# Output rows read back in five and three head pairs, and the last half row tile in two quarters

## The chip, the cores and the metric

The kernel runs on one core of one Trainium2 chip. The metric is the device time of one execution in microseconds (us), shown as the median of several runs. One execution is also recorded by the hardware profiler; the trace and the profile page come from it.

## The reference

The kernel computes a trunk of two hybrid encoder layers on 1024 rows of 1024 columns. Three groups of attention heads (A, B, C) run on column slices of one projection; each group's output is multiplied by its gate, all are joined to 1024 columns, and one output projection maps them back. A last RMSNorm closes the trunk.

```python
def rms_norm(x, g):
    y = xf * lax.rsqrt(jnp.mean(xf * xf, axis=-1, keepdims=True) + EPS)
    return (y * g.astype(jnp.float32)).astype(x.dtype)
...
    oc = mla_blocks(qc_nope, qc_rope, kc_nope, kc_rope, vc, (C_NOPE + C_ROPE) ** -0.5) * jax.nn.silu(cg)
    o = jnp.concatenate([oa, ob, oc], axis=-1)
    return x + jnp.einsum('bsm,md->bsd', o, w_out)
...
    return rms_norm(h, final_g)
```

The change lies in the `einsum` with `w_out` (for both layers) and in the last `rms_norm`.

## The kernel before

**Precision.** A product of two float32 matrices is made as three matmuls in a rounded format: each operand is split into a high part (a cast) and a low part (a subtraction), and high × high, high × low and low × high are added in PSUM (`mm3`, L133 to L136). So every tile that is multiplied needs a cast, mostly on ACT or POOL, and a subtraction on DVE, before it can be used in full.

**The output projection.** Attention writes its results to a scratch array in HBM, `d_o`, in eight head pairs of 128 (A 0 to 2, B 3 to 5, C 6 and 7). The projection reads them back by row tile `st` of 128 rows (eight of them): `out_rows` (L1016) loads some pairs of one tile, or of two, into `ol`; `out_hl` (L1025) makes the high part `oh` on ACT (L1029) and turns `ol` into the low part on DVE (L1030). In the kernel before a row tile has pairs 0 to 5 in one tile (768 columns, two buffers) and pairs 6 and 7 of two row tiles in another (one buffer). The weights Wo are eight tiles, one for a head pair, each loaded in two halves `wost` and split into `woh` and `wol` (`load_wo`, L1041): 0 to 4 (`MW = 5`) during the last part of attention, 5 to 7 in a second pool when attention's keys have been given up (L1219). For each row tile and each half of 512 output columns, `out_part` (L1053) adds 8 pairs × 3 matmuls into one PSUM tile `pw`.

**What runs when.** `ab_done` (L997) runs while group C's last units are still under way. It loads row tiles 0 and 1 and Wo's first five tiles, and the first four `out_part`s, pairs 0 to 4, are woven into the end of attention as filler work (L1209). Behind that the loop over row tiles (L1227) finishes these halves with pairs 5 to 7, adds the residual `y` on DVE (L1238), loads row tile `st + 2`, and in layer 0 begins the next layer's norm, in layer 1 the last RMSNorm.

**The end of attention.** The last group of C (`c_1_6`, rows 6 and 7 of head pair 7) makes two products with the values, `poc_1_6_0_1` and `poc_1_6_1_1` (16 matmuls of 256 columns each), in one PSUM bank, the O bank: `pv` (L752) multiplies, ACT copies half of the bank (`ohc`, L763), and DVE adds the other half to it (`oc`, L1156). Only then is the bank free for the next product. The finished group is multiplied by its gate on POOL and written to `d_o` (`finish`, L1121).

**What sets the order.** Each engine works through its own list in order, and waits on semaphores. Where the code doesn't pin two instructions to each other, a scheduler with a model of the times chooses the order in each list when the kernel is built (`schedule_with_timeline_sim=True`, L1346). All loads and stores without an engine of their own go through SP's queue (L97); `queue_behind` (L98) keeps them behind a given earlier one. Behind Wo's last half, SP is given the broadcast of the next norm's weights (`ng`; in the last layer `fg`, 128 copies of a row, 512 KB) and the loads for the row tiles from 2 on.

Of the kernel before, what the change touches and what calls it, by code (L numbers as in the profile page):

```python
# [8 lines left out]
F32 = mybir.dt.float32  # L9
F32R = mybir.dt.float32r  # L10
AF = mybir.ActivationFunctionType
ALU = mybir.AluOpType
# [4 lines left out]
EPS = 1e-6  # L17
# [8 lines left out]
MW = 5  # L26
# [19 lines left out]
def kernel(  # L46
# [21 lines left out]
    nc = tc.nc  # L68
    P = 128
    S, D = x.shape[1], x.shape[2]  # L70
    DEPTH = norm_g.shape[0]
    NS = S // P
# [5 lines left out]
    small = ctx.enter_context(tc.tile_pool(name="small", bufs=4))  # L78
# [37 lines left out]
    V, G, A, T = Engine(nc.vector), Engine(nc.gpsimd), Engine(nc.scalar), Engine(nc.tensor)  # L116
# [111 lines left out]
    for l in range(DEPTH):  # L228
        x_src = xin if l == 0 else x_next[l - 1]
        last = l == DEPTH - 1  # L230
# [16 lines left out]
        with stage.ph as ph:  # L247
# [16 lines left out]
            def gemm_sc(ws, st, name):  # L264
                his, los, n = ws
                hf, c0 = st // 4, (st % 4) * P
                ps = ps_o(name)
                for dt in range(ND):
                    wh, wl = his[dt], los[dt]
                    h, lo = hTh[hf][:, dt, c0 : c0 + P], hTl[hf][:, dt, c0 : c0 + P]  # L270
                    mm3(ps[:, :n], [(h, wh), (h, wl), (lo, wh)], dt == 0, dt == ND - 1)
                return ps
# [144 lines left out]
            for st in range(NS):  # L417
                nm = f"{l}_{st}"
                ps = gemm_sc(ws, st, f"pza{nm}")
# [7 lines left out]
                ss = small.tile([P, 8], F32, tag="ss8", name=f"ssa{nm}")  # L427
# [33 lines left out]
            for st in range(NS):  # L461
                nm = f"{l}_{st}"
                ps = gemm_sc(ws_b, st, f"pzb{nm}")
# [216 lines left out]
        wa_ = ExitStack()  # L680
        queue_behind[0] = stage.last_w
        with ExitStack() as ph:
# [314 lines left out]
            def ab_done():  # L997
                pk_.close()
                vp_.close()
                wa_.oo = wa_.enter_context(tc.tile_pool(name=f"oo{l}", bufs=1, side="right", reuse_waits="tile"))  # L1000
                wa_.wa = wa_.enter_context(tc.tile_pool(name=f"wa{l}", bufs=1, side="right", reuse_waits="tile"))
                for st in range(2):
                    out_rows(0, 6, st)
                for m in range(MW):
                    load_wo(wa_.wa, m)
                    if m == 0:
                        x_row(0)
                for st in range(2):
                    out_hl(0, 6, st)
                x_row(1)  # L1010
                out_rows(6, 8, 0, 2)
                out_hl(6, 8, 0)

            orows, xrows, wo_ins = {}, {}, {}

            def out_rows(m0, m1, st, n=1):  # L1016

                lo = wa_.oo.tile(
                    [P, m1 - m0, n * P], F32R, tag=f"ol{m0}", name=f"ol{l}_{st}_{m0}", bufs=1 if m0 else 2
                )  # L1020
                wo_ins["o"] = dma(lo, d_o[:, m0:m1, st * P : (st + n) * P])
                for i in range(n):
                    orows[m0, st + i] = lo[:, :, i * P : (i + 1) * P]

            def out_hl(m0, m1, st):  # L1025

                lo = orows[m0, st]
                h = wa_.oo.tile([P, m1 - m0, P], F32R, tag=f"oh{m0}", name=f"oh{l}_{st}_{m0}", bufs=1 if m0 else 2)
                A.copy(h, lo.bitcast(F32))  # L1029
                V.tensor_sub(lo, lo.bitcast(F32), h.bitcast(F32))  # L1030
                for m in range(m0, m1):
                    orows[m, st] = h[:, m - m0, :], lo[:, m - m0, :]
# [8 lines left out]
            def load_wo(pool, m, hi_eng=None):  # L1041
                wa_.w[m] = hi, lo = [pool.tile([P, D], F32R, name=f"wo{t}{l}_{m}") for t in "hl"]
                for c in range(2):
                    cs = slice(c * 512, (c + 1) * 512)
                    st_ = wa_.wa.tile([P, 512], F32, tag="wost", name=f"wost{l}_{m}_{c}", bufs=WST)
                    wo_ins[0] = dma(st_, w_out[l, m * P : (m + 1) * P, cs])
                    if hi_eng is A:
                        A.copy(hi[:, cs], st_)
                    else:
                        G.tensor_scalar(hi[:, cs], st_, 1.0, 0.0, ALU.mult, ALU.add)  # L1050
                    V.tensor_sub(lo[:, cs], st_, hi[:, cs].bitcast(F32))

            def out_part(st, c, m0, m1):  # L1053

                if m0 == 0:
                    wa_.ps[st, c] = (ps_o if (2 * st + c) % 4 == 3 else ps_s)(f"pw{l}_{st}_{c}")
                cs = slice(c * 512, (c + 1) * 512)
                for m in range(m0, m1):
                    h, lo = orows[m, st]
                    wh, wl = (t[:, cs] for t in wa_.w[m])  # L1060
                    mm3(wa_.ps[st, c], [(h, wh), (h, wl), (lo, wh)], m == 0, m == 7)
                    yield
# [153 lines left out]
        with ExitStack() as ph:  # L1216
            ph.enter_context(wa_)
            wb = ph.enter_context(tc.tile_pool(name=f"wb{l}", bufs=1, side="right", reuse_waits="tile"))
            for m in range(MW, 8):  # L1219
                load_wo(wb, m, A)  # L1220
            queue_behind[0] = wo_ins[0]
            if last:
                fg = wb.tile([P, D], F32, name="fg", bufs=1)
                dma(fg, final_g.partition_broadcast(P))
            else:
                dma(stage.ng, norm_g[l + 1].partition_broadcast(P))
            for st in range(NS):  # L1227
                nm = f"{l}_{st}"
                s_ = slice(st * P, (st + 1) * P)
                y = xrows[st]  # L1230
                if last:
                    ss = small.tile([P, 2], F32, tag="ss2", name=f"ssf{nm}")
                for c in range(2):
                    cs = slice(c * 512, (c + 1) * 512)
                    for _ in out_part(st, c, MW if (st, c) in wa_.ps else 0, 8):
                        pass
                    ps = wa_.ps[st, c]
                    V.tensor_add(y[:, cs], ps, y[:, cs])  # L1238
                    if last:
                        jk = wb.tile([P, 512], F32, tag="jk", name=f"jkf{nm}_{c}", bufs=2)  # L1240
                        A.activation(jk, y[:, cs], AF.Square, accum_out=ss[:, c : c + 1])
                        if c == 0:
                            e0 = small.tile([P, 1], F32, tag="e0", name=f"e0{nm}")
                            V.tensor_scalar(e0, ss[:, 0:1], 1.0 / D, EPS, ALU.mult, ALU.add)
                            V.tensor_mul(y[:, cs], y[:, cs], fg[:, cs])
                if st < NS - 2:
                    out_rows(0, 6, st + 2)
                    out_hl(0, 6, st + 2)
                    if st % 2:
                        out_rows(6, 8, st + 1, 2)  # L1250
                    queue_behind[0] = wo_ins["o"]
                if st < NS - 1:
                    out_hl(6, 8, st + 1)
                if last:
                    ms = small.tile([P, 1], F32, tag="ms1", name=f"ms_f{nm}")
                    V.scalar_tensor_tensor(ms, ss[:, 1:2], 1.0 / D, e0, ALU.mult, ALU.add)
                    r = small.tile([P, 1], F32, tag="rs1", name=f"rs_f{nm}")
                    G.tensor_tensor(out=r, in0=ms, in1=mhalf[:, 0:1], op=ALU.pow)
                    tc.keep_in_program_order(nc.vector.tensor_mul(y[:, 512:1024], y[:, 512:1024], fg[:, 512:1024]))
                    A.activation(y[:, 0:512], y[:, 0:512], AF.Copy, scale=r[:, 0:1])  # L1260
                    dma(x_dst[s_, 0:512], y[:, 0:512], nc.scalar)
                    V.tensor_scalar(y[:, 512:1024], y[:, 512:1024], r[:, 0:1], None, ALU.mult)
                    dma(x_dst[s_, 512:1024], y[:, 512:1024])
                    if st < NS - 2:
                        x_row(st + 2)
                    continue
                dma(x_dst[s_, :], y)
                if not last:
                    xt = stage.px.tile([P, D], F32, tag="xt", name=f"xt{l + 1}_{st}", bufs=XTB)
                    stage.norm(st, xt, y, xt)  # L1270
                    if st == WV_ST:
                        stage.load_wv()
                    if st < NS - 1:
                        stage.turn(st, xt, ps_t)
                    else:
                        stage.xt = xt
                    if st < NS - 2:
                        x_row(st + 2)
# [72 lines left out]
```

## Time and profile before

| | |
|---|---|
| median of 3 runs | 1325.95 us (1325.19 to 1326.66) |
| the profiled execution | 1325.05 us, span of the trace 1323.3 us |
| granted TensorE clock, mean over the span | 0.996 of full speed |
| PE busy | 1294.8 us, 98% |
| DVE, ACT, POOL busy | 882.6, 720.7, 530.2 us |
| the chain that ended last, by engine | PE 84%, DVE 5%, ACT 4%, DMA 3%, issue 2% |

The profile is one execution on the hardware. PE is the matmul unit, DVE the vector engine, ACT the scalar engine, POOL GpSimd, SP the queue that issues transfers. The page's first part gives each engine's busy time. The chain that ended last is followed back from the last instruction, at each step to what released it: a piece that names PE is time in which PE's own work set the end, a piece that names a DMA or another engine is time in which PE stood and waited for it. A timeline lists the instructions of one engine by start; a number in brackets is the idle time before one and what ended it. A matmul's recorded duration includes its way through the array; matmuls follow each other closer than that, so their rate is read from their starts. In names such as `ol_2_0` the first number is the row tile and the second the first head pair; the trace's rows leave the numbers out.

### The profile page before, as it was taken

How to read it: one execution, taken by the hardware profiler on the slowest of the kernel's cores; microseconds unless marked ns; L12 is line 12 of the kernel's file. 1: busy time of each engine (PE TensorE's matmuls, PEld its weight loads, DVE VectorE, ACT ScalarE, POOL GpSimd, SP SyncE). 2: the span in 40 equal slices, each digit the busy share in tenths (PEclk: the TensorE clock that was granted, in tenths of full speed). 3: DMA queues.
4: the chain of work that ended last, by engine and by line, in shares of the span. 5: the costliest groups of instructions: out<-in, count | busy, mean ns of one | idle time of the engine just before them, and what ended most of it. 6: DMA issues, size and time to landing. Idle time of an engine off the chain costs nothing.

```text
span 1323.3 us, 21690 instructions
## 1 busy us (share of the span) xinstructions
PE 1294.8 (98%) x7320; PEld 1131.1 (85%) x7320; DVE 882.6 (67%) x2242; ACT 720.7 (54%) x1551; POOL 530.2 (40%) x602
## 2 busy tenths in 40 slices
PE   7999999999999999999999999999999999999997
PEld 7888998878998998878898889888798988888786
DVE  5685662058888988875537766600888899888543
ACT  4332341168888898842323224311888889887332
POOL 3430121026766666751114101200367776677210
PEclk8999999999999999999999999999999999999999
DMA  7244469255211431345523345791742226114443
GB/s 255 89 125 150 136 203 258 89 140 142 82 49 56 115 90 47 108 144 177 186 91 115 121 134 157 237 221 55 180 102 61 72 64 149 38 40 148 147 146 115
DMA packets 174702, 166.46 MB, mean 126 GB/s; under 512 B 22400, under 2 KB 147200, under 8 KB 174592
## 3 DMA queue, kind: packets, MB, share of 16 engines
q1 hardware_dynamic: 155840, 140.43, 37.3%
q10 hardware_dynamic: 18752, 24.65, 5.4%
q8 instruction: 58, 0.95, 0.3%
q14 instruction: 52, 0.43, 0.1%
HBM read 107.35 MB, written 57.67 MB: 125 GB/s over the span
## 4 chain that ended last, share of the span: by engine, by line
PE 84%; DVE 5%; ACT 4%; DMA 3%; issue 2%; POOL 1%; SPq 1%; POOLq 0%; DVEq 0%; ACTq 0%
PE pg L136 13%; PE pw L136 12%; PE pzb L114 7%; PE pza L114 7%; PE poa L136 6%; PE ppa L730 5%; PE pzc L136 5%; PE sa L136 5%; PE sc L136 4%; PE ppc L730 4%; PE poc L136 3%; PE sb L136 2%; PE pob L136 2%; PE pzv L114 2%; PE pzv L136 2%
## 5 line engine op out<-in xcount | busy, mean ns | idle before, releaser
L711 DVE CUSTOM_DVE_ANT_0 pa<-sa,zero 128x512 f32<-128x512 f32 x96 | 65.5, 682 | 140.2 <-PE sa L136 137.1
L738 POOL TENSOR_SCALAR ptha<-pfa 128x512 fp32r<-128x512 f32 x96 | 59.8, 624 | 207.8 <-ACT pfa L737 199.7
L739 POOL TENSOR_TENSOR ptla<-pfa,ptha 128x512 fp32r<-128x512 f32 x96 | 124.1, 1293 | 5.7
L136 PE MATMUL sa<-ka,qsta 128*128 128x512 f32 x384 | 124.5, 418 | 1.4 <-DVE nmxc L711 0.7
L721 ACT ACTIVATE pa<-pa,nmxa 128x1024 f32<-128x1024 f32 x96 | 111.4, 1161 | 8.8 <-DVE nmxa L711 8.8
L136 PE MATMUL sc<-k,qc 128*128 128x512 f32 x384 | 113.2, 411 | 0.0
L730 PE MATMUL ppa<-ident,pa 128*128 128x128 f32 x768 | 106.5, 273 | 0.2
L730 PEld LDWEIGHTS ppa<-ident,pa 128*128 128x128 f32 x768 | 91.5, 141 | 15.1 <-DVE ptlb L742 0.6
L136 PE MATMUL pw<-woh,oh 128*128 128x512 f32 x256 | 98.9, 395 | 3.4 <-ACT oh L1029 2.6
L136 PE MATMUL pg<-hTh,wh 128*128 128x512 f32 x256 | 100.4, 392 | 0.0
L136 PE MATMUL pg<-hTh,wl 128*128 128x512 f32 x256 | 100.1, 391 | 0.0
L136 PE MATMUL pg<-hTl,wh 128*128 128x512 f32 x256 | 100.1, 391 | 0.0
L136 PE MATMUL pw<-wol,oh 128*128 128x512 f32 x256 | 99.7, 392 | 0.1
L136 PE MATMUL pw<-woh,ol 128*128 128x512 f32 x256 | 97.9, 393 | 0.3 <-DVE ol L1030 0.3
L644 ACT ACTIVATE g<-pg 128x512 f32<-128x512 f32 x32 | 19.1, 598 | 137.3 <-PE pg L136 107.0
L218 POOL TENSOR_SCALAR wh<-wst 128x384 fp32r<-128x384 f32 (+1 forms) x52 | 30.6, 607 | 145.5 <-PE pzb L114 79.2
L136 PE MATMUL poa<-ptha,vAB 128*128 128x384 f32 x256 | 88.0, 344 | 0.9 <-POOL ptla L739 0.3
L136 PE MATMUL poa<-ptla,vAB 128*128 128x384 f32 x256 | 86.5, 338 | 0.0
L721 ACT ACTIVATE pc<-pc,nmxc 128x1024 f32<-128x1024 f32 x64 | 74.0, 1156 | 8.2 <-DVE nmxc L711 8.0
L136 PEld LDWEIGHTS sc<-k,qc 128*128 128x128 f32 x384 | 66.3, 189 | 8.6
L711 DVE CUSTOM_DVE_ANT_0 pa<-sa,zero,nmxa 128x512 f32<-128x512 f32 x96 | 71.2, 744 | 3.4 <-PE sa L136 0.7
L730 PE MATMUL ppc<-ident,pc 128*128 128x128 f32 x512 | 71.9, 273 | 1.5 <-ACT pfc L737 0.8
(234 smaller groups left out, 3812.6 us busy)
## 6 DMA issues: line engine op xcount, KB each, us to landing
wst<-in_w_in_dram SPq DMA_DIRECT2D x20, 512.0 KB, 3.7
d_gate<-g ACTq DMA_DIRECT2D x32, 256.0 KB, 2.0
wost<-in_w_out_dram SPq DMA_DIRECT2D x32, 256.0 KB, 2.7
wst<-in_w_in_dram SPq DMA_DIRECT2D x16, 384.0 KB, 4.2
qsta<-d_qa SPq DMA_DIRECT2D x64, 96.0 KB, 2.8
qstb<-d_qb SPq DMA_DIRECT2D x64, 96.0 KB, 2.8
k<-d_kn SPq DMA_DIRECT2D x12, 512.0 KB, 7.0
qc<-d_qc SPq DMA_DIRECT2D x96, 64.0 KB, 2.2
```

The lines of the kernel that those rows point to most:

```text
L114: return lambda *a, **k: tc.keep_in_program_order(f(*a, **k))
L136: T.matmul(ps, lhsT=a, rhs=b, start=first and i == 0, stop=last and i == len(parts) - 1)
L218: G.tensor_scalar(h, f, 1.0, 0.0, ALU.mult, ALU.add)
L644: A.activation(g, ps, AF.Silu)
L711: V.tensor_tensor_reduce(p[:, c * 512 : (c + 1) * 512], ps, zero[:, 0:1].to_broadcast([P, 512]), -1.0, nmx[0][:, 0:1] if c else 3.0e38, AL ...
L721: A.activation(p, p, AF.Exp, scale=-1.0, bias=nmx[1][:, 0:1], accum_out=sm)
L730: T.transpose(pt[:, (j - q0) * P : (j - q0 + 1) * P], p[:, j * P : (j + 1) * P], ident)
L738: G.tensor_scalar(hi, f, 1.0, 0.0, ALU.mult, ALU.add)
L739: G.tensor_tensor(out=lo, in0=f, in1=hi.bitcast(F32), op=ALU.subtract)
```

## The change

Row tiles are split as Wo's tiles are, at `MW = 5`: pairs 0 to 4 in the tile with two buffers (640 columns), pairs 5 to 7 of two row tiles in the tile with one. The last row tile of the last layer is made in three pieces of columns, 512, 256 and 256, in place of 512 and 512: `out_part` takes the columns, and the sums of squares take a third column.

```diff
--- before.py
+++ after.py
@@ -1000,16 +1000,16 @@
                 wa_.oo = wa_.enter_context(tc.tile_pool(name=f"oo{l}", bufs=1, side="right", reuse_waits="tile"))
                 wa_.wa = wa_.enter_context(tc.tile_pool(name=f"wa{l}", bufs=1, side="right", reuse_waits="tile"))
                 for st in range(2):
-                    out_rows(0, 6, st)
+                    out_rows(0, MW, st)
                 for m in range(MW):
                     load_wo(wa_.wa, m)
                     if m == 0:
                         x_row(0)
                 for st in range(2):
-                    out_hl(0, 6, st)
+                    out_hl(0, MW, st)
                 x_row(1)
-                out_rows(6, 8, 0, 2)
-                out_hl(6, 8, 0)
+                out_rows(MW, 8, 0, 2)
+                out_hl(MW, 8, 0)
 
             orows, xrows, wo_ins = {}, {}, {}
 
@@ -1050,11 +1050,12 @@
                         G.tensor_scalar(hi[:, cs], st_, 1.0, 0.0, ALU.mult, ALU.add)
                     V.tensor_sub(lo[:, cs], st_, hi[:, cs].bitcast(F32))
 
-            def out_part(st, c, m0, m1):
-
+            def out_part(st, c, m0, m1, cs=None):
+
+                cs = cs or slice(c * 512, (c + 1) * 512)
                 if m0 == 0:
-                    wa_.ps[st, c] = (ps_o if (2 * st + c) % 4 == 3 else ps_s)(f"pw{l}_{st}_{c}")
-                cs = slice(c * 512, (c + 1) * 512)
+                    ps = (ps_o if (2 * st + c) % 4 == 3 else ps_s)(f"pw{l}_{st}_{c}")
+                    wa_.ps[st, c] = ps[:, 0 : cs.stop - cs.start]
                 for m in range(m0, m1):
                     h, lo = orows[m, st]
                     wh, wl = (t[:, cs] for t in wa_.w[m])
@@ -1229,34 +1230,40 @@
                 s_ = slice(st * P, (st + 1) * P)
                 y = xrows[st]
                 if last:
-                    ss = small.tile([P, 2], F32, tag="ss2", name=f"ssf{nm}")
-                for c in range(2):
-                    cs = slice(c * 512, (c + 1) * 512)
-                    for _ in out_part(st, c, MW if (st, c) in wa_.ps else 0, 8):
+                    ss = small.tile([P, 3], F32, tag="ss3", name=f"ssf{nm}", bufs=2)
+                cuts = [0, 512, 768, 1024] if last and st == NS - 1 else [0, 512, 1024]
+                nc_ = len(cuts) - 1
+                for c in range(nc_):
+                    cs = slice(cuts[c], cuts[c + 1])
+                    for _ in out_part(st, c, MW if (st, c) in wa_.ps else 0, 8, cs):
                         pass
                     ps = wa_.ps[st, c]
                     V.tensor_add(y[:, cs], ps, y[:, cs])
                     if last:
-                        jk = wb.tile([P, 512], F32, tag="jk", name=f"jkf{nm}_{c}", bufs=2)
+                        jk = wb.tile([P, 512], F32, tag="jk", name=f"jkf{nm}_{c}", bufs=2)[:, 0 : cs.stop - cs.start]
                         A.activation(jk, y[:, cs], AF.Square, accum_out=ss[:, c : c + 1])
-                        if c == 0:
-                            e0 = small.tile([P, 1], F32, tag="e0", name=f"e0{nm}")
-                            V.tensor_scalar(e0, ss[:, 0:1], 1.0 / D, EPS, ALU.mult, ALU.add)
+                        if c < nc_ - 1:
+                            e1 = small.tile([P, 1], F32, tag=f"e{c}", name=f"e{c}{nm}", bufs=2)
+                            if c:
+                                V.scalar_tensor_tensor(e1, ss[:, c : c + 1], 1.0 / D, e0, ALU.mult, ALU.add)
+                            else:
+                                V.tensor_scalar(e1, ss[:, 0:1], 1.0 / D, EPS, ALU.mult, ALU.add)
+                            e0 = e1
                             V.tensor_mul(y[:, cs], y[:, cs], fg[:, cs])
                 if st < NS - 2:
-                    out_rows(0, 6, st + 2)
-                    out_hl(0, 6, st + 2)
+                    out_rows(0, MW, st + 2)
+                    out_hl(0, MW, st + 2)
                     if st % 2:
-                        out_rows(6, 8, st + 1, 2)
+                        out_rows(MW, 8, st + 1, 2)
                     queue_behind[0] = wo_ins["o"]
                 if st < NS - 1:
-                    out_hl(6, 8, st + 1)
+                    out_hl(MW, 8, st + 1)
                 if last:
                     ms = small.tile([P, 1], F32, tag="ms1", name=f"ms_f{nm}")
-                    V.scalar_tensor_tensor(ms, ss[:, 1:2], 1.0 / D, e0, ALU.mult, ALU.add)
+                    V.scalar_tensor_tensor(ms, ss[:, nc_ - 1 : nc_], 1.0 / D, e0, ALU.mult, ALU.add)
                     r = small.tile([P, 1], F32, tag="rs1", name=f"rs_f{nm}")
                     G.tensor_tensor(out=r, in0=ms, in1=mhalf[:, 0:1], op=ALU.pow)
-                    tc.keep_in_program_order(nc.vector.tensor_mul(y[:, 512:1024], y[:, 512:1024], fg[:, 512:1024]))
+                    tc.keep_in_program_order(nc.vector.tensor_mul(y[:, cs], y[:, cs], fg[:, cs]))
                     A.activation(y[:, 0:512], y[:, 0:512], AF.Copy, scale=r[:, 0:1])
                     dma(x_dst[s_, 0:512], y[:, 0:512], nc.scalar)
                     V.tensor_scalar(y[:, 512:1024], y[:, 512:1024], r[:, 0:1], None, ALU.mult)
```

The scheduler's lists change with it. The following pieces are from layer 0; layer 1 has the same order with other numbers (`fg` for `ng`). In the names, `ohc_1_6_0_1` is the copy of the O bank after the last but one product, `oc_1_6` the tile of the last C group, `oh_2_0` and `ol_2_0` the high and low part of row tile 2.

ACT, when it has cast the last of Wo (tile 7), before the change:

```order
L1048 CAST woh_7_7389<-wost_7_0_7391 128x512
L1048 CAST woh_7_7389<-wost_7_1_7395 128x512
L763 COPY ohc_1_6_0_1_7287<-poc_1_6_0_1_7220 64x256
L1029 CAST oh_2_0_7422<-ol_2_0_7420 128x768
L1029 CAST oh_1_6_7425<-ol_0_6_6866 128x256
L162 ACTIVATE xt_0_7429,ss_0_7430<-y_0_6816 128x1024
```

and with it:

```order
L1048 CAST woh_7_7389<-wost_7_0_7391 128x512
L1048 CAST woh_7_7389<-wost_7_1_7395 128x512
L1029 CAST oh_2_0_7422<-ol_2_0_7420 128x640
L763 COPY ohc_1_6_0_1_7287<-poc_1_6_0_1_7220 64x256
L1029 CAST oh_1_5_7425<-ol_0_5_6866 128x384
L162 ACTIVATE xt_0_7429,ss_0_7430<-y_0_6816 128x1024
```

The cast of row tile 2 has moved from behind the O bank's copy to ahead of it.

DVE at the same place, behind the same Wo tile, before:

```order
L1051 TENSOR_TENSOR wol_7_7390<-wost_7_1_7395,woh_7_7389 128x512
L1156 TENSOR_TENSOR oc_1_6_7052<-poc_1_6_0_1_7220,ohc_1_6_0_1_7287 64x256
L1238 TENSOR_TENSOR y_0_6816<-pw_0_0_7223,y_0_6816 128x512
L1030 TENSOR_TENSOR ol_2_0_7420<-ol_2_0_7420,oh_2_0_7422 128x768
L1238 TENSOR_TENSOR y_0_6816<-pw_0_1_7267,y_0_6816 128x512
L1030 TENSOR_TENSOR ol_0_6_6866<-ol_0_6_6866,oh_1_6_7425 128x2x128
```

and with it:

```order
L1051 TENSOR_TENSOR wol_7_7390<-wost_7_1_7395,woh_7_7389 128x512
L1030 TENSOR_TENSOR ol_2_0_7420<-ol_2_0_7420,oh_2_0_7422 128x640
L1157 TENSOR_TENSOR oc_1_6_7052<-poc_1_6_0_1_7220,ohc_1_6_0_1_7287 64x256
L1241 TENSOR_TENSOR y_0_6816<-pw_0_0_7223,y_0_6816 128x512
L1241 TENSOR_TENSOR y_0_6816<-pw_0_1_7267,y_0_6816 128x512
L1030 TENSOR_TENSOR ol_0_5_6866<-ol_0_5_6866,oh_1_5_7425 128x3x128
```

The subtraction for row tile 2 has moved from behind the addition `oc` that frees the O bank, and behind a residual addition `y`, to ahead of both.

SP's queue behind Wo's last halves, before:

```order
L97 DMA wost_7_0_7391<-in_w_out_dram 128x512
L97 DMA wost_7_1_7395<-in_w_out_dram 128x512
L97 DMA d_o_86<-oc_1_3_6714 128x384
L97 DMA ng_7365<-in_norm_g_dram 128x1024
L97 DMA ol_2_0_7420<-d_o_86 128x6x128
L97 DMA x_69<-y_0_6816 128x1024
```

and with it:

```order
L97 DMA wost_7_0_7391<-in_w_out_dram 128x512
L97 DMA wost_7_1_7395<-in_w_out_dram 128x512
L97 DMA ng_7365<-in_norm_g_dram 128x1024
L97 DMA ol_2_0_7420<-d_o_86 128x5x128
L97 DMA d_o_86<-oc_1_3_6714 128x384
L97 DMA x_69<-y_0_6816 128x1024
```

The broadcast and the load of row tile 2 have moved ahead of the write of C's last but one group to `d_o`.

## Rows read from the trace of the kernel before

**Rows 1.** The page, part 1: busy us, share of the span, instructions.

```profile
PE 1294.8 (98%) x7320; PEld 1131.1 (85%) x7320; DVE 882.6 (67%) x2242; ACT 720.7 (54%) x1551; POOL 530.2 (40%) x602
```

**Rows 2.** The chain that ended last, end of layer 0's attention: start us, us, what.

```profile
586.36 6.22 DMA ol<-d_o
...
592.60 0.84 ACT oh L1029
...
593.48 9.45 PE pw L136 x40
```

**Rows 3.** The same chain, end of layer 1's attention.

```profile
1237.37 5.31 DMA ol<-d_o
...
1242.69 0.84 ACT oh L1029
...
1243.56 0.97 DVE ol L1030
...
1244.57 61.05 PE pw L136 x268
```

**Rows 4.** Timeline, 584 to 590 us, SP's queue: start us, issue us, engine, line.

```profile
584.64 0.33 SPq L97 DMA_DIRECT2D wost<-in_w_out_dram  x1
585.52 0.33 SPq L97 DMA_DIRECT2D d_o<-oc  x1
585.89 0.42 SPq L97 DMA_DIRECT2D ng<-in_norm_g_dram  x1
```

**Rows 5.** Timeline, 1234.9 to 1240 us, SP's queue.

```profile
1235.05 0.33 SPq L97 DMA_DIRECT2D wost<-in_w_out_dram  x1
1235.93 0.33 SPq L97 DMA_DIRECT2D d_o<-oc  x1
1236.30 1.02 SPq L97 DMA_DIRECT2D fg<-in_final_g_dram  x1
```

**Rows 6.** DMA issues of both stretches: count, KB, median us from issue to landing.

```profile
ng<-in_norm_g_dram SPq DMA_DIRECT2D x1, 512.0 KB, 5.5
...
fg<-in_final_g_dram SPq DMA_DIRECT2D x1, 512.0 KB, 5.2
```

**Rows 7.** Timeline, 588.9 to 594.6 us, PE: first and last of 16 poc matmuls.

```profile
589.77 0.28 PE L136 MATMUL poc<-pthc,vC 128*128 128x256 f32 x1
...
591.57 0.28 PE L136 MATMUL poc<-ptlc,vC 128*128 128x256 f32 x1
```

**Rows 8.** Timeline, 584 to 600 us, DVE.

```profile
588.47 0.41 DVE L1156 TENSOR_TENSOR oc<-poc,ohc 64x256 f32<-64x256 f32 x1
...
594.94 0.42 DVE L1030 TENSOR_TENSOR ol<-ol,oh 128x256 fp32r<-128x256 f32 x1
```

**Rows 9.** Loads of tile ol, 1195 to 1324 us.

```profile
DMA to landing us min/median/max: 3.3/3.8/8.8
```

**Rows 10.** Timeline, 1236 to 1248 us, ACT.

```profile
1244.06 0.39 ACT L1029 CAST oh<-ol 128x256 fp32r<-128x256 f32 x1
```

**Rows 11.** Timeline, 1314 to 1324 us, DVE.

```profile
1316.53 0.69 DVE L1238 TENSOR_TENSOR y<-pw,y 128x512 f32<-128x512 f32 x1 [1.62 <-PE pw L136]
```

**Rows 12.** Timeline, 1239.6 to 1246 us, PE; in brackets the idle time before.

```profile
1243.58 0.50 PE L136 MATMUL pw<-woh,oh 128*128 128x512 f32 x1 [0.99 <-ACT oh L1029]
```

**Rows 13.** Timeline, 1314 to 1324 us, ACT.

```profile
1317.25 0.63 ACT L1241 ACTIVATE jkf<-y 128x512 f32<-128x512 f32 x1 [3.13 <-DVE y L1238]
```

**Rows 14.** Timeline, 5 to 20 us, PE; in brackets the idle time before.

```profile
8.93 1.09 PE L114 MATMUL pt<-ident,xt 128*128 128x128 f32 x8 [1.83 <-DVE xt L114]
14.69 1.97 PE L114 MATMUL pt<-ident,xt 128*128 128x128 f32 x8 [4.67 <-DVE xt L114]
```

**Rows 15.** The chain that ended last, 14 to 30 us.

```profile
16.65 4.13 PE pzv L114 x24
```

**Rows 16.** Windows: busy us by engine, then granted clock, DMA share, GB/s.

```profile
13.00:20.00 7.00, 5.31 (x27) 5.32 (x28) 5.25 (x7) 3.37 (x6) 4.26 (x5) 0.54 0.93 347
...
590.00:600.00 10.00, 8.36 (x44) 6.91 (x43) 4.87 (x7) 2.55 (x5) 1.30 (x2) 1.00 0.29 98
```

## The prediction

> **What bounds the kernel now.** I read the page first: TensorE (PE) is busy for 98% of the span [rows 1], so time can only be won or lost where PE waits or where its instruction count changes. The diff touches the last stage of each layer, so the second view is the chain of waits around its start. In both layers the chain leaves PE there for one transfer, the load of row tile 2 (`ol<-d_o`), and returns over the ScalarE (ACT) cast `oh` [rows 2] and, in layer 1, also the VectorE (DVE) subtraction `ol` [rows 3]. After that PE runs to the end of the program without another piece of the chain that is a wait on a load: 268 matmuls in 61.05 us, 0.228 us each [rows 3]. So a microsecond by which this load's consumers are late is a microsecond of the result.
>
> Third, the queue that issues the load. On SP a Wo half is issued at 584.64, then the write `d_o<-oc` at 585.52 (it waited for its operand, since the issue before it ended at 584.97), then the broadcast `ng` at 585.89 and the load at 586.36 [rows 2, 4]. Layer 1 has the same order with `fg` [rows 3, 5]. The broadcast lands 5.5 us after its issue, 591.4, and the load behind it 1.2 us later, at 592.58 [rows 2, 6]. In layer 1: 1241.5 and, again 1.2 later, 1242.68 [rows 3, 6].
>
> Fourth, PE itself. While the load is under way, PE does the last attention product `poc` (16 matmuls of 256 columns, 589.77 to 591.57, 0.12 us each) without waiting, and stands still after it until 593.48, where the chain resumes [rows 2, 7]. That product needs the one O bank, which is free once ACT has copied and DVE has added the previous product: 0.41 us on DVE at 588.47, long before the load lands [rows 8].
>
> **The change part by part.**
>
> *The order of ACT and DVE.* Output rows 2 to 7 now come in five and three pairs, and with them the scheduler's order changes, as the pieces of order ahead show: on ACT the cast of row tile 2 stands ahead of the copy `ohc` of the O bank, on DVE its subtraction ahead of the `oc` addition that frees the bank. Both engines run in order. So `poc`, which needed nothing of the load, now waits for the load, its cast, its subtraction and the addition. The three matmuls of pair 5 of `pw_1_0`, which ran before `poc`, now come behind `pw_2_0`'s first ones, because pair 5 of row tile 1 moved to the later load.
>
> *Landing.* SP issues the load before the write `d_o<-oc`, not after it. Without the write the broadcast can go at 585.01 (584.64 + 0.33 and a gap of 0.04), 0.88 earlier, and the same sum in layer 1 gives 0.88 too (1235.42 for 1236.30) [rows 4, 5]. The load carries 320 KB for 384; five sixths of the 1.2 us behind the broadcast is 1.0. Landing: 592.58 − 0.88 − 0.2 = 591.5, and 1242.68 − 1.08 = 1241.6. Bounds: no earlier than before (592.6, 1242.7) if the transfer rate decides and not the issue; and 3.3 us after issue, the shortest of this load's kind [rows 9], that is 588.8 and 1239.8. I take the middle because both layers show the load 1.2 us behind the broadcast. The write goes half a microsecond or so later than before; its readers are the loads from row tile 3 on, which SP issues three and more transfers later, so I count nothing for it.
>
> *From landing to PE.* The cast of 640 columns lies between 0.39 (256 columns) and 0.84 (768) [rows 2, 10], by columns 0.73; the subtraction between 0.42 [rows 8] and 0.97 [rows 3], by columns 0.83; the addition 0.41 [rows 8]. `ohc` on ACT lies beside the subtraction. With gaps of 0.02 to 0.04 that is 2.0 us from landing to the first `poc`. Then 16 × 0.12 = 1.92 [rows 7], so `pw_2_0` starts 3.92 us after landing. Behind the addition on DVE wait the two `y` additions of row tile 0, which free PSUM banks; at 0.69 each [rows 11] they end while `poc` and the first matmuls run, so they cost nothing as long as that cover of 1.92 us stands.
>
> *Layer 0.* 591.5 + 3.92 = 595.42 against 593.48 [rows 2]: 1.94 late, and the 3 moved matmuls still to do, 3 × 0.228 = 0.68. Loss 2.6 us. By the bounds of the landing −0.1 to +3.7.
>
> *Layer 1.* There PE had done two matmuls of `pw_2_0`, from 1243.58 on, before it stood again for `ol`; the third began at 1244.57 [rows 3, 12]. Now 1241.6 + 3.92 = 1245.52, plus those two and the three moved ones, 5 × 0.228 = 1.14: 1246.66 against 1244.57, loss 2.1 us; by the bounds +0.2 to +3.2.
>
> *Everything gained earlier.* Smaller casts for row tiles 0 and 1 may let PE reach this place some tenths sooner; it then waits that much longer for the landing, so I count nothing. *The loads of three pairs* (single buffer) for row tiles 3, 5, 7 replace those of two pairs. PE has the first five pairs of two halves, 30 matmuls or 6.8 us, between the release of the buffer and its next use; a load of 3.3 to 3.8 us [rows 9], and a cast and subtraction under 0.6 each, fit. If that cover is short, PE waits for `ol` in row tile 3 or 5.
>
> *The quarters.* The last half's 24 matmuls of 512 columns become 48 of 256: 48 × 0.12 − 24 × 0.228 = +0.3 us [rows 3, 7]. What follows the last matmul works on 256 columns for 512: the DVE addition falls from 0.69 to some 0.42 and the ACT square from 0.63 to some 0.4 [rows 8, 10, 11, 13], −0.5. Net −0.2; bounds +0.3 (if nothing after it shortens) and −0.5. What the first quarter adds (an addition, a square, a small step, a product) lies beside the second quarter's 24 × 0.12 = 2.9 us. The Trainium skill, "TensorE: Matmul & The Clock Gate", Part 1 ("Wait — 56ns, not 53.3ns?"), says that warm matmuls start N ÷ 2.4 GHz plus about 2.5 ns apart; by it the 48 would cost only 48 × 0.109 − 24 × 0.216 = +0.06 us, and the net would be −0.4. The rows are slower than that rule at both widths, and the sum keeps them.
>
> **Sum.** 2.6 + 2.1 − 0.2 = +4.5 us. The profiled execution took 1325.05 us (its span is 1323.3), which becomes 1329.5; the median of the runs shown, 1325.95, is 0.9 above it, so I predict 1330.4 us. What can be told from no change is about 0.2%, 2.65 us.
>
> **Rivals.**
>
> *Early landing.* With the write gone from ahead of it, the load comes as an ordinary load of its kind does, 3.3 to 3.8 us after issue [rows 9]: 589.0 and 1240.0 on average. Losses 0.1 and 0.5, less 0.2: about 1326.3, no change. To come under 2.65 us the two landings together must be 1.9 us earlier than I forecast. For it: the median of row loads. Against: in both layers the 512 KB broadcast lies ahead in the queue, and the load ended 1.2 us after it each time. The same result if the change does not do what it says, in that SP's issue and not the buffer release bound the load.
>
> *Faster: PE never waits.* If the cast and the subtraction end before PE gets to `poc`, the new order is harmless and the old stalls vanish. PE gets there three matmuls sooner, 589.77 − 0.68 = 589.1 [rows 7]; the load must have landed 2.0 earlier, at 587.1, 1.6 us after its issue. Then layer 0 gains its stand of 1.8 us (591.57 + 0.12 to 593.48) and, if layer 1 is counted alike, the two and the quarters make −3.8: 1322.2. It decides for faster where the landings together are 7.1 us earlier than I forecast (4.5 + 2.65); the shortest load on record allows 4.5 of these [rows 9]. Only a load that finds the queue empty could do it, and the broadcast stands ahead of it.
>
> *The clock falls.* PE's stand grows from 1.8 us to some 4.4 in layer 0 (589.1 to 593.5), and in layer 1 by about as much. In the program's first 20 us PE stood 4.67 us before 14.69, and the granted clock was 0.54 in the stretch from 13 to 20 us, near its lower level of 1.2 GHz; after a stand of 1.83 us the same 8 transposes took 1.09, after 4.67 us 1.97, and the next 24 matmuls of 256 columns 4.13 us for 24 × 0.12 = 2.88 [rows 14 to 16]. Together 2.1 us. One such loss gives 1332.5, two 1334.6. Before, the stand of 1.8 us in 590 to 600 left the clock at 1.00 [rows 16]. For it: 4.4 is close to 4.67; against: the early stretch is busy with small pieces on both sides of its stand, while here PE is full until the stand. The Trainium skill, same page, Part 1 ("What's actually happening"), has the throttled clock as the default that activity releases, so that standing still brings the low level; the rows of the start agree, and no row here shows a stand of 4.4 us behind full work.
>
> *Late landing.* The transfers are limited by rate and the load is no earlier than before: losses 3.7 and 3.2 less 0.2, 1332.6.
>
> **How the numbers follow.** Forecast 0.52; early landing or no effect 0.18; clock 0.17; late landing 0.08; faster 0.05. So slower by over 0.2% is 0.52 + 0.17 + 0.08 = 0.77, within it 0.18, faster 0.05. The range goes from 1326.0, which takes in most of the early landings, to 1334.0, which takes in late landing and one fall of the clock, with the two falls left out: about 0.8.
>
> **What would show it.** Right: in the changed profile the load is issued ahead of `d_o<-oc` near 585.5 and 1236.5 and lands near 591.5 and 1241.6; `poc`'s 16 matmuls start about 2 us after that, with PE's wait before them put down to DVE `oc` and its chain to the load; no stand between `poc` and `pw_2_0`; and the last half ends 0.3 us later relative to its start while its tail is 0.5 shorter. Wrong: `poc` starting at 589 to 590 as before (the order does not hold it), a load that lands by 589, a clock under 1.00 after the stand, or a new stand before pair 5 in row tiles 3 to 7.

## The result, and the profile after

The changed kernel takes 1334.91 us (median of 6 runs, 1332.77 to 1336.65) against 1326.31 for the kernel before in the same comparison (1325.15 to 1328.77). The ratio is 1.0066, with a 95% interval of 1.0055 to 1.0076: slower by 0.0066 × 1326.31 = 8.75 us, with an interval of 7.3 to 10.1 us. The forecast was 4.5 us slower, and the measured median lies 0.9 us above the end of the range. The profiled execution has a span of 1333.7 us and a mean granted clock of 0.992.

The chain that ended last, at the end of layer 0's attention (start, us, what); it answers to [rows 2]:

```profile
584.94 0.33 SPq L97
...
585.32 0.42 SPq L97
...
585.80 5.70 DMA ol<-d_o
...
591.57 0.73 ACT oh L1029
...
592.33 0.83 DVE ol L1030
593.15 0.34 DVE oc L1157
...
593.54 3.79 PE poc L136 x16
```

The load lands at 585.80 + 5.70 = 591.50, and `poc` starts 2.04 us later, behind the cast, the subtraction and the addition. Before, the chain went from the cast straight to `pw`, and `poc` wasn't in it.

The timeline of PE at that place, with the idle time before an instruction in brackets; it answers to [rows 7]:

```profile
589.26 0.40 PE L136 MATMUL pw<-woh,ol 128*128 128x512 f32 x1
593.54 0.58 PE L136 MATMUL poc<-pthc,vC 128*128 128x256 f32 x1 [3.88 <-DVE oc L1157]
593.91 0.42 PE L136 MATMUL poc<-ptlc,vC 128*128 128x256 f32 x1
594.13 0.42 PE L136 MATMUL poc<-pthc,vC 128*128 128x256 f32 x1
...
596.91 0.41 PE L136 MATMUL poc<-ptlc,vC 128*128 128x256 f32 x1
597.12 0.63 PE L136 MATMUL pw<-woh,oh 128*128 128x512 f32 x1
597.55 0.63 PE L136 MATMUL pw<-wol,oh 128*128 128x512 f32 x1
...
599.56 0.63 PE L136 MATMUL pw<-woh,oh 128*128 128x512 f32 x2
600.03 0.40 PE L136 MATMUL pw<-wol,oh 128*128 128x512 f32 x1
```

PE stands for 4.05 us (593.54 − 589.26, less 0.23 for the matmul ahead), where it stood for 1.8 before. Then there is something new: `poc`'s matmuls start 0.21 us apart where they started 0.12 apart, and `pw`'s 0.43 apart where 0.228 was usual, until 599.56. Windows of both layers show the granted clock behind the stand (busy us of PE, PEld, DVE, ACT, POOL, then the clock, DMA share and GB/s):

```profile
590.00:600.00 10.00, 6.46 (x24) 5.87 (x25) 4.67 (x8) 3.03 (x6) 2.19 (x2) 0.66 0.17 65
1246.00:1256.00 10.00, 6.39 (x27) 5.31 (x28) 5.74 (x12) 4.45 (x10) 1.65 (x2) 0.83 0.15 48
```

Before, the clock in 590 to 600 was 1.00 [rows 16]. In layer 1 the chain has the same form: the load is issued 5.5 us later in the program than before, and lands 6.1 us later. The rows answer to [rows 3]; the last two are from the chain of a longer window:

```profile
1242.89 5.91 DMA ol<-d_o
...
1248.88 0.73 ACT oh L1029
...
1249.64 0.83 DVE ol L1030
1250.46 0.34 DVE oc L1157
...
1250.84 3.40 PE poc L136 x16
1254.24 62.19 PE pw L136 x273
```

PE at that place, the first matmul of `poc`, the first of `pw`, and the first that is at full rate again:

```profile
1250.84 0.39 PE L136 MATMUL poc<-pthc,vC 128*128 128x256 f32 x1 [2.67 <-DVE oc L1157]
...
1254.04 0.63 PE L136 MATMUL pw<-woh,oh 128*128 128x512 f32 x1
...
1254.83 0.39 PE L136 MATMUL pw<-woh,ol 128*128 128x512 f32 x1
```

At the end of the program the effect of the quarters is visible. These rows are DVE, ACT and POOL behind the last matmul, which starts at 1327.34 (before: 1316.10); the first two answer to [rows 11] and [rows 13]:

```profile
1327.65 0.42 DVE L1241 TENSOR_TENSOR y<-pw,y 128x256 f32<-128x256 f32 x1 [0.83 <-PE pw L136]
```

```profile
1328.17 0.42 ACT L1244 ACTIVATE jkf<-y 128x256 f32<-128x256 f32 x1 [2.14 <-DVE y L1241]
...
1330.40 0.34 ACTq L97 DMA_DIRECT2D out_dram<-y  x1
```

```profile
1328.95 0.66 POOL L1265 TENSOR_TENSOR rs_f<-ms_f,mhalf 128x1 f32<-128x1 f32 x1 [7.70 <-DVE ms_f L1263]
```

The row of POOL in the kernel before:

```profile
1318.24 0.93 POOL L1258 TENSOR_TENSOR rs_f<-ms_f,mhalf 128x1 f32<-128x1 f32 x1 [9.83 <-DVE ms_f L1256]
```

From the last matmul's start to the issue of ACT's last store it is 3.06 us, where the kernel before has these two rows, 3.86 us apart:

```profile
1316.10 0.39 PE L136 MATMUL pw<-woh,ol 128*128 128x512 f32 x1
```

```profile
1319.96 0.34 ACTq L97 DMA_DIRECT2D out_dram<-y  x1
```

### The profile page after: what moved, and what is told of

Read it like the earlier page. It is cut to its first block, busy times and chain, and to the rows that moved or that the text cites. A ratio compares the mean times of both kernels' runs of the same rounds, so it can differ in the third digit from the quotient of the medians.

```text
span 1333.7 us, 21748 instructions
## 1 busy us (share of the span) xinstructions
PE 1301.4 (98%) x7344; PEld 1135.8 (85%) x7344; DVE 884.0 (66%) x2245; ACT 720.7 (54%) x1553; POOL 529.4 (40%) x602
## 4 chain that ended last, share of the span: by engine, by line
PE 80%; DVE 7%; DMA 4%; ACT 3%; POOL 3%; issue 3%; SPq 0%; POOLq 0%; DVEq 0%; ACTq 0%
PE pg L136 13%; PE pw L136 9%; PE pzb L114 7%; PE pza L114 7%; PE poa L136 6%; PE ppa L730 5%; PE sc L136 5%; PE pzc L136 4%; PE sa L136 4%; PE ppc L730 3%; PE poc L136 3%; DVE pa L711 2%; PE pob L136 2%; PE pzv L114 2%; PE sb L136 2%
## 5 line engine op out<-in xcount | busy, mean ns | idle before, releaser
L136 PE MATMUL pw<-woh,oh 128*128 128x512 f32 (+1 forms) x264 | 101.6, 392 | 1.7 <-ACT woh L1048 0.9
L136 PE MATMUL pw<-wol,oh 128*128 128x512 f32 (+1 forms) x264 | 102.1, 389 | 0.3 <-DVE wol L1051 0.2
L136 PE MATMUL pw<-woh,ol 128*128 128x512 f32 (+1 forms) x264 | 98.9, 386 | 0.0
```

Source lines behind the costliest of these rows:

```text
L136: T.matmul(ps, lhsT=a, rhs=b, start=first and i == 0, stop=last and i == len(parts) - 1)
```

## The experiments

The theory after the result, **A**: the order on ACT and DVE (cast and subtraction of row tile 2 ahead of the O bank's copy and addition) makes `poc` wait for the load, PE stands for 4.05 us in layer 0 and 2.83 in layer 1, and the stand brings the clock down for what follows; the loss is about half stand, half clock. Rival **B**: the time is lost in the transfers (the load's new place, the three-pair tiles, late Wo halves in layer 1). Rival **C**: the clock falls for another reason than the stand. The kernels were timed in three groups, each beside runs of the kernel before on the same chip; ratios are to these.

### The old order by hand, everything else as changed

Two orders without a semaphore are added to `out_hl`; `obank` holds the copies and additions of the O bank as they are issued.

```diff
-                A.copy(t[:, :n], po[64:128, :n])
+                obank.append(A.copy(t[:, :n], po[64:128, :n]).ins)
...
-                A.copy(h, lo.bitcast(F32))
-                V.tensor_sub(lo, lo.bitcast(F32), h.bitcast(F32))
+                hi_ = A.copy(h, lo.bitcast(F32))
+                lo_ = V.tensor_sub(lo, lo.bitcast(F32), h.bitcast(F32))
+                if m0 == 0 and st == 2:
+                    after(hi_.ins, obank[-4])
+                    after(lo_.ins, obank[-3])
```

> The changed kernel, with two orders added by hand: in both layers ACT casts row tile 2 behind the O bank's copy of the last but one product, and DVE subtracts it behind the addition that frees the bank. Everything else, the load's place ahead of the write too, stays. Theory A (that order alone makes PE stand, and the stand drops the clock): poc's 16 matmuls start at about 589 in layer 0 without a wait for oc, PE stands about 1.3 us behind them instead of 4.05, the granted clock stays at 1.00 in 590 to 600 (0.66 in the changed kernel) and in the same place of layer 1, and the time is that of before within 1 us, 1325.5 to 1327.5. Rival B (the loss lies in the transfers, the 320 KB load ahead of the write or the late Wo halves of layer 1): the time stays above 1331, with PE waiting for landings. Rival C (the clock falls for another reason than the stand): the stand is gone, the clock still drops, 1329 to 1331.

Measured: 1326.57 us, before 1325.94, ratio 1.0002 (0.9991 to 1.0013). The loss is gone. What PE waits for in 583 to 600 us (total, times, longest), and the clock:

```profile
PE pw L137 <- ACT woh L1052: 0.8, 1, 0.8
PE pw L137 <- ACT oh L1030: 0.7, 1, 0.7
PE pw L137 <- DVE y L1245: 0.3, 1, 0.3
```

```profile
590.00:600.00 10.00, 8.94 (x45) 7.15 (x44) 5.56 (x8) 2.55 (x5) 1.30 (x2) 1.00 0.30 107
```

`poc` waits for nothing any more, and the clock stays at 1.00, in layer 1 too. The split, the three-pair loads and the load's new place on SP are all still in this kernel, so rival B falls as the cause of the 8.75 us. The interval, −1.2 to +1.7 us, leaves room for a small cost of theirs (see what stays open).

### The split without the quarters

```diff
-                cuts = [0, 512, 768, 1024] if last and st == NS - 1 else [0, 512, 1024]
+                cuts = [0, 512, 1024]
```

> The changed kernel without the quarters: the last half row tile is made in one piece of 512 columns again. All theories: the quarters are worth 0.2 us, so 1334.9 to 1335.3; the stands of 4 and 2.8 us and the clock's fall in both layers as in the changed kernel. If the quarters themselves cost something in the last row tiles, this run is over 1 us faster.

Measured: 1335.71 us, ratio 1.0074 (1.0056 to 1.0091). That overlaps with the changed kernel's interval, so nothing shows that the quarters carry a part of the loss, and what they are worth lies below what these runs tell. The waits on `oc` are there again, 2.6 and 2.2 us in this profile (3.9 and 2.7 in the changed kernel's), and so is the lower clock, 0.83 and 0.66 in the two windows.

### Work for PE while it stands

```diff
+                    if (st, c) == (0, 1):
+                        fl = ps_t(f"fl{l}")
+                        end = mms[-1]
+                        for k in range(12):
+                            f = T.matmul(fl, lhsT=wa_.w[1][0][:, 0:P], rhs=wa_.w[0][0][:, 0:512], start=k == 0, stop=k == 11)
+                            after(f.ins, end)
+                            end = f.ins
+                        after(opart[0], end)
```

`opart[0]` is `poc`'s first matmul; a list of further orders holds PE's row behind it as the changed kernel has it.

> The changed kernel with 12 matmuls of 512 columns on Wo's tiles into a spare PSUM tile, their result unused, put on PE between pw_0_1 and poc in both layers; the order behind them is held as it is in the changed kernel. They take 12 x 0.227 = 2.7 us of the 4.05 us that PE stands in layer 0 and of the 2.83 in layer 1, and nothing waits for them. Theory A (half of the loss is the clock, which falls because PE stands): poc still starts 2 us behind the landing, but at full rate, 0.12 us each; the granted clock stays 1.00; 2.6 us less in layer 0 and 1.7 less in layer 1: 1330 to 1331.5. Rival C (the clock falls for another reason): no less time, 1334 to 1336, clock as low as in the changed kernel.

Measured: 1330.14 us, ratio 1.0029 (1.0018 to 1.0041). PE at the place in layer 0, and both windows:

```profile
589.34 2.90 PE L1264 MATMUL fl<-woh,woh 128*128 128x512 f32 x12
593.59 0.39 PE L141 MATMUL poc<-pthc,vC 128*128 128x256 f32 x1 [1.35 <-DVE oc L1170]
593.82 0.28 PE L141 MATMUL poc<-ptlc,vC 128*128 128x256 f32 x1
593.93 0.28 PE L141 MATMUL poc<-pthc,vC 128*128 128x256 f32 x1
```

```profile
590.00:600.00 10.00, 8.65 (x46) 7.16 (x45) 4.67 (x8) 2.96 (x6) 1.30 (x2) 1.00 0.25 88
1246.00:1256.00 10.00, 8.73 (x47) 7.55 (x47) 5.76 (x13) 4.01 (x11) 1.68 (x2) 1.00 0.20 65
```

`poc` starts at 593.59, as late as in the changed kernel (593.54), but at full rate. Twelve matmuls in each layer that compute nothing of use make the kernel faster: what is left of the loss is 0.0029 × 1325.94 = 3.8 us, the wait; the other 4.9 of the 8.75 is the clock (the two losses have intervals of about ±1.5 us each). Rival C falls: what the edit changed is work for PE during the wait, and the clock stayed up.

### The order of before, and the load ahead of the broadcast

As in the first experiment, and `out_rows(0, MW, 2)` is called before the broadcast is issued; with five pairs the tile's buffer is free by then.

```diff
             queue_behind[0] = wo_ins[0]
+            out_rows(0, MW, 2)
+            queue_behind[0] = wo_ins["o"]
             if last:
...
-                    out_rows(0, MW, st + 2)
+                    if st:
+                        out_rows(0, MW, st + 2)
```

> As e1_pinned, and the load of row tile 2 is issued ahead of the broadcast (ng, fg), right behind Wo's last half; the five pairs' buffer is free by then. Theory A with the landing 3.3 to 3.8 us behind its issue at about 585.3: landing near 589, the cast at 589.7 and the subtraction at 590.5, before poc is done at 591; PE doesn't stand at all in either layer, 1.8 and 1.6 us less than before and 0.2 from the quarters: 1322 to 1323.5. Rival B (the transfers' rate, not the order in the queue, sets the landing): it lands as late as in the changed kernel and the time is that of e1_pinned.

Measured: 1324.28 us, ratio 0.9984 (0.9975 to 0.9994). The load lands 3.4 us behind its issue at 585.16, as expected, and 4.6 us behind it in layer 1. The waits at this place are gone: 0.2 and 0.3 us are left, for Wo's tiles. The gain, 2.1 us, is smaller than the 3.6 expected (1.8, 1.6 and 0.2 for the quarters). Which part fell short isn't settled.

### The changed order, with the load ahead of the broadcast

The edit of `out_rows` above alone.

> The changed kernel with only the load moved: row tile 2's five pairs are issued right behind Wo's last half, ahead of the broadcast; ACT's and DVE's orders stay as the change has them (in layer 1 two of row tile 1's instructions swap places with their neighbours). Theory A (the order costs as much as the load is late: poc starts 2.0 us behind the landing): landing near 588.6 and 1239.7 as in e5_pinned_early, poc at 590.6 instead of 593.5, PE stands 1.4 us in layer 0 and about as long in layer 1, the clock stays 1.00; less the stand in front of pw_2_0, which falls away: 1324.5 to 1326.5, no slower than before. A rival by which the order costs its stand and the clock wherever the load lands: 1330 or more.

Measured: 1326.67 us, before 1326.55, ratio 0.9997 (0.9986 to 1.0007). The order is the one that cost 8.75 us, and with the earlier load the kernel is no slower than before. Beside the old order with the same load (the experiment before this one, ratio 0.9984) it is 0.0013, some 1.7 us, behind. The chain in layer 0:

```profile
588.63 0.72 ACT oh L1029
...
589.38 0.83 DVE ol L1030
590.21 0.34 DVE oc L1157
...
590.59 2.16 PE poc L136 x16
```

`poc` still starts 2.0 us behind the landing, but the landing (588.54) is 3.0 us earlier; PE stands for 1.0 and 1.1 us and the clock stays at 1.00. So it is order and landing together that set the price, as the prediction's sum has it.

### The kernel before, with the changed order

`out_hl`'s orders reversed in the kernel before (the copy behind the cast, the addition behind the subtraction), and `pw_2_0` held behind `poc`.

```diff
+                if m0 == 0 and st == 2:
+                    after(obank[-4], hi_.ins)
+                    after(obank[-3], lo_.ins)
...
+                    if (st, c) == (2, 0):
+                        after(mms[k], olast[0])
```

> The kernel before, its six and two pairs, SP order and halves kept, with the change's order forced on: ACT copies the O bank behind the cast of row tile 2, DVE frees it behind the subtraction, and pw_2_0 stays behind poc. Theory A (the order alone is enough, without the split): landing at 592.6 and 1242.7 as before, poc 2.3 us behind it, PE stands about 5 us in layer 0 and 3 to 4 in layer 1, less two matmuls that come in between; stand 2.9 and 2.4 us worse than before, and the clock falls in both layers, 2 to 2.6 each: 1334 to 1338. Rival (the split itself costs, by its loads and three-pair tiles): 1326 to 1329.

Measured: 1335.53 us, ratio 1.0062 (1.005 to 1.0074). The longest waits of the two layers, and the windows:

```profile
PE pw L139 <- ACT oh L1033: 4.3, 1, 4.3
```

```profile
PE pw L139 <- DVE oc L1163: 4.8, 1, 4.8
```

```profile
590.00:600.00 10.00, 7.46 (x29) 6.63 (x30) 4.07 (x7) 3.02 (x6) 2.34 (x2) 0.66 0.13 53
1246.00:1256.00 10.00, 6.10 (x27) 5.58 (x28) 4.45 (x10) 3.93 (x9) 1.68 (x2) 0.66 0.16 57
```

Two matmuls of `pw` stand ahead of `poc` in PE's list here, and the wait is put down to them; in layer 0 they wait for the cast of pairs 6 and 7, which stands behind the cast of row tile 2 and the O bank's copy on ACT (592.08, 0.40 us). Six and two pairs and the new order give the loss; five and three pairs and the old order don't. Neither the split nor the quarters is needed for it.

### The kernel before, with the broadcast behind the load

`bc` is the broadcast of `ng` or `fg`; one order is added, and no other engine's list changes.

```diff
                 if st < NS - 2:
                     out_rows(0, 6, st + 2)
+                    if st == 0:
+                        after(bc, wo_ins["o"])
```

> The kernel before with one thing changed: the broadcast (ng, fg) goes behind the load of row tile 2 on SP; all other engines keep their order. Theory A (the broadcast ahead of the load sets the landing, and the landing the stand): the load lands 3.4 to 4.6 us behind its issue, near 589.4 and 1240.5, is cast and subtracted by 591.2 and 1242.5, when poc ends; the stands of 1.8 and 1.6 us go: 1322.5 to 1324. Rival (the transfers' rate sets the landing): 1325.5 to 1326.5.

Measured: 1321.93 us, before 1326.55, ratio 0.996 (0.9947 to 0.9972): the fastest of the study, 13 us under the changed kernel by the medians and half a microsecond under what was expected. SP in layer 0, and what PE still waits for in 583 to 600 us:

```profile
584.06 0.33 SPq L97 DMA_DIRECT2D wost<-in_w_out_dram  x1
584.94 0.33 SPq L97 DMA_DIRECT2D d_o<-oc  x1
585.32 0.42 SPq L97 DMA_DIRECT2D ol<-d_o  x1
585.78 0.63 SPq L97 DMA_DIRECT2D ng<-in_norm_g_dram  x1
```

```profile
PE pw L136 <- ACT oh L1029: 0.2, 1, 0.2
```

In layer 1 nothing is left in the list. The load took 5.2 us in layer 0, more than expected, and lands at 590.5, early enough for `poc` to cover most of its cast.

### The quarters alone, and with the swap

> The kernel before with the quarters alone, six and two pairs kept. From the tails of the profiles (last matmul's start to the last store's issue 3.86 us before, 3.06 in the changed kernel) less 0.3 us of added matmul time: 0.5 us less than before, 1325 to 1326, which these rounds may not tell from no change; the tail in its profile is 3.0 to 3.1 us. If the quarters carried a part of the loss: over 1327.

The change's last part on the kernel before, with six and two pairs (its small tiles with one buffer each). Measured: 1326.82 us, before 1326.55, ratio 1.0002 (0.999 to 1.0014). The tail is as expected, 1319.17 to 1322.24 in its profile, 3.07 us for 3.86; a gain of half a microsecond can't be told from these runs.

The same profile shows something else. Its order on ACT and DVE is that of before, but the load of row tile 2 took 6.85 us in layer 0 (6.22 in the profile of before), PE stood for 2.5 us instead of 1.8, and the clock fell; eight matmuls of `pw` from 595.37 on started 0.43 us apart:

```profile
594.04 0.50 PE L136 MATMUL pw<-woh,oh 128*128 128x512 f32 x1 [2.33 <-ACT oh L1029]
```

```profile
590.00:600.00 10.00, 7.67 (x34) 6.12 (x33) 4.25 (x6) 2.55 (x5) 1.29 (x2) 0.83 0.27 95
```

So the clock falls behind a stand in the old order too, when the landing is late enough.

> The kernel before with both things that the runs so far favour: the broadcast behind the load of row tile 2 on SP (e8, 4.6 us less in its rounds), and the last half row tile in quarters (0.8 us less behind the last matmul, 0.3 more matmul time). Theory A: the two add up, stands as in e8 and a tail of 3.1 us, 0.5 us less than e8's gain: ratio 0.9955 to 0.9965, 1321 to 1322. If the quarters disturb the order near the end or the broadcast comes too late for the first norm of the next stage, the ratio is 0.997 or more.

Both together, measured: 1322.51 us, before 1326.18, ratio 0.9969 (0.9958 to 0.9981), a little over the 0.9955 to 0.9965 expected. The interval overlaps with that of the swap alone; nothing shows that the quarters add to it.

## Why the prediction was wrong

**The order, right.** `poc` waits for the load's landing, cast, subtraction and the addition, 2.04 us behind the landing where 2.0 was worked out; cast 0.73 and subtraction 0.83 as interpolated. The changed kernel with the old order by hand, and the kernel before with the changed order, show that this order makes the difference, in both directions.

**The landing, right in layer 0, less so in layer 1.** In layer 0 it is 591.50 for 591.5, partly by luck: the broadcast was issued 0.3 us later than worked out (585.32 for 585.01) and landed sooner behind its issue, 5.1 us for 5.5. In layer 1 the load took 5.91 us from issue to landing where the prediction's sum gives 5.1 (5.31 − 0.2), so it is 0.8 us later than counted, beside what layer 0 had delayed already.

**The stand, right.** 4.5 us was the sum, with 0.2 for the quarters taken off. With the clock held up by fillers the kernel is 3.8 us slower than before (2.4 to 5.4 by the interval). By rows, `pw_2_0` of layer 0 starts at 597.12 for 593.48, 3.64 us later, of which 1.66 are `poc` at the lower clock; with the three moved matmuls that is 2.7 us for the 2.6 worked out.

**The clock, the step that failed.** The prediction opened with the statement that time can only be won or lost where PE waits or where its instruction count changes; the rate at which PE works was left out. It had the fall of the clock as a rival with a chance of 0.17 and put it at nothing in the sum, on the argument that PE is full until the stand here, unlike in the program's first stretch. The clock fell in both layers, which is one of the prediction's own signs of being wrong. In layer 0 `poc` took 593.54 to 597.12, 3.58 us for 1.92, and the six matmuls behind it to 599.56 took 2.44 for 6 × 0.228 = 1.37: 2.7 us. In layer 1 `poc`'s 16 took 3.20 (1250.84 to 1254.04) and two of `pw` 0.79 for 0.46: 1.6 us. Together 4.3 us by rows, 4.9 by the runs with fillers; the rival's price was 2.1 a layer, 4.2 for two. That the total fits is in part luck, since neither layer paid 2.1; what was wrong is that the sum held nothing for it and the chance was low. The row against it, a stand of 1.8 us at 1.00, said nothing about one of 4 us; the nearest row was the one of 4.67 us, with the clock at 0.54 around it [rows 14, 16], and the estimate should have gone by it. That PE was full until the stand did not keep the clock up. The Trainium skill, "TensorE: Matmul & The Clock Gate", Part 1 ("What's actually happening"), calls the throttled clock the default that activity releases; by that rule the stand alone is enough, and the experiment with fillers agrees: 0.66 and 0.83 without them, 1.00 with them.

**The range.** It left out the case that came, two falls (1334.6 by the prediction's own price). The measured median is 1334.91.

**The quarters.** The tail shortened by 0.8 us, not 0.5: besides the addition (0.69 to 0.42) and the square (0.63 to 0.42), POOL's `pow` (tile `rs_f`) took 0.66 for 0.93. No run tells the net from nothing.

**What stays open.** The load ahead of the broadcast gained 5.3 us with six and two pairs and 2.1 with five and three and the old order, and the two intervals don't overlap, though the two profiles have spans of 1320.3 and 1320.9 and neither shows a stand of half a microsecond at this place. What makes their medians differ isn't shown by these profiles; a cost of the split elsewhere, of some of these 3.2 us, isn't excluded. The gain of 5.3 us is also more than the 3.4 us that PE stood in the one profile of before (1.8 in layer 0, 1.2 and 0.4 in layer 1). The profile of the quarters alone, with a longer stand and a fall of the clock in the old order, suggests that other executions of the kernel before lose more there than its profile shows; that is argued, not shown. Why the scheduler chose the other order for five and three pairs isn't shown by any run either.

## What to carry to other kernels

When a scheduler sets the order, look in its lists for an instruction that waits for a transfer and now stands ahead of one that frees a buffer or a bank; its price is the landing time plus what lies between, and can be read from the trace of before. Then price what the engine's idleness does afterwards: stands of TensorE of 2.83 and 4.05 us were paid twice here, once as the wait and once as half rate behind it. And look at what else is in the queue ahead of the load that everyone waits for: putting one broadcast behind it won 5.3 us, where the change lost 8.75.

## What the runs showed that was not expected

Stands and the clock behind them, each read at the end of attention in one layer from the starts of PE's matmuls: 1.0 and 1.1 us (changed order, early load), 1.4 and 1.5 (with fillers), and 1.8 (before) left the granted clock at 1.00; 2.4 and 2.8 (without the quarters), 2.5 (the quarters alone), 2.8 and 4.05 (changed kernel), 4.5 and 4.96 (the kernel before with the changed order) were followed by windows of 0.66 to 0.83. The fall can come after PE has taken up work again: in layer 1 of the changed kernel `poc`'s first matmuls still started 0.12 us apart and the slow ones began half a microsecond after the restart, and in the kernel with the quarters alone they began 1.3 us after it.

POOL's `pow` of one column, the same instruction, took 0.93 us while DVE multiplied 512 columns beside it (before), and 0.66 us while DVE multiplied 256 (changed kernel, and the quarters alone).

The load of 320 KB for row tile 2 landed 3.1 to 4.6 us after its issue when the broadcast of 512 KB was behind it on the queue (two kernels, both layers), and 4.9 to 6.1 us after it when the broadcast was ahead (four kernels, both layers).
